# A hybrid convolution and attention layer on one core: another order of the first phase, and gate weights loaded beside the conv input

## The chip, the cores and the metric

The kernel runs on one core of a Trainium2 chip. The metric is the device time of one execution in microseconds (us). Before the change it was 634.33 us in the median of 3 runs (632.48 to 634.84). One further execution was recorded instruction by instruction; the profile and the trace are of that one.

The engines of the core, as the profile names them: PE (TensorE, matrix products; PEld is its weight load), DVE (VectorE), ACT (ScalarE), POOL (GpSimd) and SP (SyncE, which issues nearly all DMA transfers here). Each engine works through its own list of instructions in order. An instruction that waits holds back everything behind it on its engine, on SP a DMA issue as well.

## The reference

One layer with D = 1024, 1024 latent tokens (x) and 256 context tokens (ctx), all in float32:

```python
mod = silu(c) @ w_ada + b_ada                 # w_ada: 1024 x 3072
shift, scale, gate = split(mod, 3)            # adaLN; shift_c, scale_c likewise from c_ctx
hl = rmsnorm(x, norm_g) * (1 + scale) + shift
hc = rmsnorm(ctx, norm_g) * (1 + scale_c) + shift_c
zl = split(hl @ w_in)                         # w_in: 1024 x 3840, 11 parts
zc = split(hc @ w_in)                         # of it only keys and values are used
ya = zl[1] * dwconv3(zl[2] * zl[0]) * silu(zl[3])
yb = neighbourhood_attention(q=zl[4], k=zl[5], v=zl[6], keys and values of zc, rpb) * silu(zl[7])
yc = silu(layernorm(dwconv31(zl[8] * sigmoid(zl[9])) + b)) * silu(zl[10])
x  = x + gate * (concat(ya, yb, yc) @ w_out)
return rmsnorm(x, final_g)
```

The attention has 8 heads of 64, a window of 8 rows by 16 columns on a grid 64 wide with a bias per relative position, and all 256 context keys in the same softmax.

## The kernel before

**Precision.** A large product is made of three: an operand is split into a high half (a rounding copy, usually on ACT) and a low half (source minus high half, on DVE or POOL), and PE sums high x high, high x low and low x high in PSUM. In the code and in the profile these halves are `wh` and `wl` for weights, `h` (two tiles) for tokens.

**Stages.** In the first phase (`start()`, to 76.3 us) tokens are normalised, turned so that channels lie on the partitions, modulated and split; the first Q and K columns are multiplied there too. After it comes the conformer convolution's input for the first 128 of its channels ("the conv input", `cf_in(0)`: two weight blocks, each for two halves of the tokens, with matmuls at L325 to L327 and sinks at L667 and L670; the K columns of the context tokens stand behind its first half); then the v product (`v_proj`, L413 to L415, ten tiles of 128 tokens, to 162 us); then attention over four pairs of heads with the remaining projections between its rows; then the output product. The change touches the order of the first phase and three start times right behind it.

**The first phase is an order written by hand.** The string `SEQ` is read from left to right, and each word calls a small function in `start()` that issues some instructions. The letter names the function, the digits are its arguments:

| word | what it issues | lines |
|---|---|---|
| X0 to X9 | load of a tile of 128 tokens, 512 KB (0 to 7 latent, 8 and 9 context) | norm_load |
| L00 to L31 | load of adaLN weights, 1 MB in two transfers; k is a quarter of the columns, g a half of the rows | ada_load |
| W00 to W11 | load of 256 KB of `w_in` into a `wr` tile: i = 0 for the first Q columns, 1 for K; g is a half of the rows | L311 |
| w00 to w11 | split of such a tile: `wh` on ACT, then `wl` on POOL | L130, L131 |
| q50, q51 | sum of squares of token tile 5, on ACT (last digit 0) or on DVE (1) | L264, L266 |
| r42 | root of the mean square for tiles 4 and 5, on POOL | L270, L272 |
| x4 | scaling of token tile 4, on DVE | L960 |
| B00, B01 | adaLN product for quarter 0 with the first and with the second half of the rows, 4 matmuls each | L221 |
| R0, C0 | copy of that row to SBUF (ACT); 4 transposes (PE) and the small DVE steps that make `shift` and `scl` of quarter 0 | L226; L233, L235 to L241 |
| a0 to a7 | 4 transposes: 128 channels of token tiles 0 to 3 (a22: into a free `ps_z` tile) | L280 |
| b0 to b7, c0 to c3 | the same for tiles 4 to 7, and for the context tiles with 2 x 128 channels | L280 |
| f, g, h | modulation on ACT after a, b, c | L295 |
| u, v, o | split of the modulated tokens after f, g, h, both halves on DVE | L301, L302 |
| m0 to m7, n0 to n7 | 6 matmuls of Q and K for 128 channels: tokens 0 to 511 (m), 512 to 1023 (n) | L1010, L1011, L1013 |
| D16 | 16 warm-up matmuls of zeros into a tile (`po`) that is not yet in use | L980 |
| O, Q00 to Q12 | the attention tiles are allocated; Q and K are copied out of PSUM | L353, L354, L372, L373 |

In this phase the lists of PE, DVE, ACT, POOL and SP all follow the string. Behind it PE keeps the order of the code, and the lists of the other four are made by the framework's scheduler from the order of the code and added dependences. The buffers that matter: ten token tiles `x_in`, two PSUM tiles `ps_h` for transposes, two `ps_a` for adaLN rows, three `ps_z`, two `wr`, four pairs `wh`/`wl`.

**Behind the first phase** three side tasks run beside the conv input. `spawn(task, delay)` starts a task once the code has written out matmuls worth `delay` us by its own count (0.65 us for three matmuls of 512 columns, `mm_k`); a task then goes on whenever its next due time on that count is reached.

- `v_weights`: four loads of the v columns of `w_in` (L399) and their splits (ACT L130, DVE L131), 3.0 apart.
- `ada_gates`: the last third of `w_ada` in 16 loads of 256 KB (L810), each followed by one multiply and add on DVE (L815) that is bound to stand behind the PE instruction last written; 1.2 apart. At the end two splits and four transfers out to DRAM (L823). Each load takes a tile `t2`, of which there are four.
- `bias_first`: the position bias, as chains of small transfers through DRAM (tiles `dpr`, `dpm`, `u`) and tables loaded from them (L503).

The v product drains each token tile out of PSUM twice, by ACT (L424) and DVE (L425) into a `t2` tile, from the same four; the tile is then sent to DRAM (`vd`). Its PSUM tile is one of the three `ps_z`. DVE also does the 31 steps of the convolution (L681, L686) in that time.

Of the kernel before, what the change touches and what calls it, by code (L numbers as in the profile page):

```python
# [49 lines left out]

SEQ = """
X0 X1 X2 X3 L00 K L01 W00 W10 L10 L11 X4 X5 X6 X7 W01 W11 L20 L21 L30 L31 X8 X9
q00 q10 r02 x0 x1 q20 q30 r22 x2 x3 D16 a0 a1 a22 D04 B00 D04 B01 R0 D03 w00 w10 C0 D06
f0 f1 a3 u0 u1 m0 m1
B10 D04 B11 R1 D03 q40 q51 C1 D04 f2 f3 u2 u3 r42 x4 x5 m2 m3 q60 q71 r62 x6 x7 D04
b0 b1 g0 v0 g1 v1 B20 n0 b2 n1 b3 w01 w11 g2 v2 g3 v3 B21 R2 n2 a4 C2 n3 a5 f4 u4 f5 u5 b4
m4 B30 m5 b5 g4 v4 B31 g5 v5 R3 n4 a6 C3 a7 n5 f6 u6 f7 u7 b6 m6 b7 g6 v6 m7 g7 v7
q80 q90 r82 x8 x9 O Q00 n6 Q01 n7
c0 c1 h0 o0 h1 o1 c2 c3 h2 o2 h3 o3 Q02 Q10 Q11 Q12
"""  # L60


# [4 lines left out]
class Builder:  # L67
# [964 lines left out]
    def build(self):  # L1032
# [50 lines left out]
        self.t2 = e(self.pool("t2", 4, side="left"))  # L1083
        self.v_alloc()
        stv = ExitStack()
        self.spawn(self.v_weights(stv.enter_context(self.pool("vw", 1, side="right"))), 8.0)
        self.spawn(self.ada_gates(), 14.0)
        self.spawn(self.bias_first(), 16.0)
        first = self.cf_in(0)
        self.run(itertools.islice(first, KT), self.proj_pair(0, self.ws[1]), first)  # L1090
        self.conv = self.cf_conv()
# [101 lines left out]
```

## Time and profile before

| | |
|---|---|
| median of 3 runs | 634.33 us (632.48 to 634.84) |
| the profiled execution | 631.35 us |
| its span, first to last instruction | 629.6 us |
| PE busy | 600.2 us, 95% of the span |
| DVE, ACT, POOL busy | 399.8, 244.5, 180.4 us |
| granted PE clock, mean | 0.986 |
| DMA moved | 78.64 MB, 125 GB/s in the mean |

How to read the rows of the prediction. A row of the time line has a start in us from the span's first instruction, a length, the engine, the line of the code, the operation, output<-inputs by the names of the tiles, shapes, and how many instructions were put together (x4); in square brackets the idle time before it and what ended it. A row of the waits gives the waiting engine, tile and line, what it waited for, and then the sum in us, the count and the longest. A row of the windows gives, for each engine, busy us and the number of instructions, then the granted PE clock (1.00 is full speed), the busy share of the DMA engines and what they moved.

### The profile page before, as it was taken

What the parts mean: (1) busy time and instruction counts of PE and PEld (TensorE: products, weight loads), DVE (VectorE), ACT (ScalarE), POOL (GpSimd) and SP (SyncE); (2) the same over time, 40 slices, a digit from 0 to 9 for tenths busy, and PEclk for the clock granted to TensorE, in tenths of its full rate; (3) what the DMA queues carried; (4) which work ended last, traced back from release to release, by engine and by line L of the source; (5) the groups of instructions that cost most, each with busy time, mean ns of one, the idle gap of its engine ahead of it and who ended that gap; (6) DMA issues with size and microseconds to landing.
All of it is one profiled execution on the core that took longest, in us unless ns stands there. A gap on an engine that the chain in (4) does not pass through costs nothing.

```text
span 629.6 us, 8940 instructions
## 1 busy us (share of the span) xinstructions
PE 600.2 (95%) x3103; PEld 499.9 (79%) x3103; DVE 399.8 (64%) x681; ACT 244.5 (39%) x469; POOL 180.4 (29%) x199
## 2 busy tenths in 40 slices
PE   5879899999999999999999999999989999999995
PEld 4456688778879888888888888888878888888885
DVE  2365786688536679767799576754879636352333
ACT  4143751121144552455433455523645444231222
POOL 1121145000032331243232324312433270265112
PEclk9999799989999999999999999999999999999998
DMA  8991165885554114523127332163221255670122
GB/s 282 356 299 51 34 230 160 157 184 145 159 132 95 48 27 142 131 48 92 38 59 192 77 98 65 30 178 95 49 69 34 83 174 178 248 281 6 69 100 101
DMA packets 97170, 78.64 MB, mean 125 GB/s; under 512 B 26507, under 2 KB 80869, under 8 KB 96997
## 3 DMA queue, kind: packets, MB, share of 16 engines
q1 hardware_dynamic: 95397, 71.51, 40.5%
q10 hardware_dynamic: 1728, 6.55, 2.9%
q8 instruction: 25, 0.41, 0.3%
q14 instruction: 20, 0.16, 0.1%
HBM read 55.93 MB, written 14.29 MB: 112 GB/s over the span
## 4 chain that ended last, share of the span: by engine, by line
PE 79%; DMA 6%; DVE 5%; issue 3%; ACT 2%; POOL 2%; SPq 2%; DVEq 0%; POOLq 0%; ACTq 0%
PE ps_z L325 12%; PE ps_z L327 12%; PE ps_z L326 12%; PE po L621 5%; PE ps_t L609 5%; PE ps_f L869 5%; PE ps_f L870 5%; PE ps_f L868 5%; PE ps_s L590 4%; PE ps_s L591 2%; DMA t<-in_w_ada 2%; PE ps_z L413 2%; PE ps_z L414 2%; PE ps_z L415 2%; PE ps_h L280 2%
## 5 line engine op out<-in xcount | busy, mean ns | idle before, releaser
L325 PE MATMUL ps_z<-h,wh 128*128 128x512 f32 x384 | 151.8, 395 | 0.0
L327 PE MATMUL ps_z<-h,wl 128*128 128x512 f32 x384 | 150.8, 393 | 0.0
L326 PE MATMUL ps_z<-h,wh 128*128 128x512 f32 x384 | 150.2, 391 | 0.0
L131 POOL TENSOR_TENSOR wl<-wr,wh 128x512 fp32r<-128x512 f32 x52 | 75.1, 1447 | 121.2 <-ACT wh L130 106.9
L600 POOL TENSOR_SCALAR pr<-pr,sm 128x640 f32<-128x640 f32 (+1 forms) x64 | 52.9, 827 | 139.6 <-DVE sm L599 118.7
L327 PEld LDWEIGHTS ps_z<-h,wl 128*128 128x128 f32 x384 | 72.3, 188 | 16.4
L686 DVE SCALAR_TENSOR_TENSOR acc<-t,half_w,acc 128x1024 f32<-128x1024 f32 x60 | 81.8, 1363 | 1.1
L326 PEld LDWEIGHTS ps_z<-h,wh 128*128 128x128 f32 x384 | 72.5, 189 | 12.5
L325 PEld LDWEIGHTS ps_z<-h,wh 128*128 128x128 f32 x384 | 72.6, 189 | 12.2
L613 ACT ACTIVATE pw<-ps_t 128x640 fp32r<-128x640 f32 (+1 forms) x64 | 43.5, 679 | 91.1 <-PE ps_t L609 91.0
L595 DVE CUSTOM_DVE_ANT_0 ps_s<-ps_s,bt 128x640 f32<-128x640 f32 (+1 forms) x64 | 51.0, 796 | 35.5 <-PE ps_s L591 34.0
L614 DVE TENSOR_TENSOR pw<-ps_t,pw 128x640 fp32r<-128x640 f32 (+1 forms) x64 | 50.4, 788 | 17.2 <-ACT pw L613 16.9
L598 ACT ACTIVATE pr<-ps_s,mn 128x640 f32<-128x640 f32 (+1 forms) x64 | 49.0, 766 | 21.5 <-DVE mn L595 20.5
L621 PE MATMUL po<-pw,vt 128*128 128x256 f32 x304 | 51.3, 297 | 2.0 <-DVE yb L572 1.1
L869 PE MATMUL ps_f<-wol,y 128*128 128x512 f32 (+1 forms) x136 | 51.6, 379 | 0.0
L870 PE MATMUL ps_f<-woh,y 128*128 128x512 f32 (+1 forms) x136 | 51.5, 379 | 0.0
L868 PE MATMUL ps_f<-woh,y 128*128 128x512 f32 (+1 forms) x136 | 51.5, 379 | 0.0
L130 ACT ACTIVATE wh<-wr 128x512 fp32r<-128x512 f32 x52 | 32.5, 629 | 34.3 <-PE ps_z L326 27.5
L590 PE MATMUL ps_s<-kt,qd 128*128 128x384 f32 (+1 forms) x128 | 42.3, 351 | 1.7 <-DMA qd<-qn 1.2
L609 PE MATMUL ps_t<-ident,pr 128*128 128x128 f32 x304 | 43.6, 272 | 0.0
L621 PEld LDWEIGHTS po<-pw,vt 128*128 128x128 f32 x304 | 40.4, 189 | 3.8 <-issue 3.4
L609 PEld LDWEIGHTS ps_t<-ident,pr 128*128 128x128 f32 x304 | 36.0, 142 | 1.8 <-issue 0.9
(170 smaller groups left out, 916.5 us busy)
## 6 DMA issues: line engine op xcount, KB each, us to landing
wr<-in_w_in SPq DMA_DIRECT2D x52, 256.0 KB
wa<-in_w_ada SPq DMA_DIRECT2D x16, 512.0 KB
qd<-qn SPq DMA_DIRECT2D x32, 256.0 KB
vd<-t SPq DMA_DIRECT2D x20, 256.0 KB
x_in<-in_x SPq DMA_DIRECT2D x8, 512.0 KB
t<-in_w_ada SPq DMA_DIRECT2D x16, 256.0 KB
vt<-vd SPq DMA_DIRECT2D x32, 128.0 KB
fraw<-in_w_out SPq DMA_DIRECT2D x8, 512.0 KB
```

Source lines behind the costliest of these rows:

```text
L131: i2 = (eng or nc.vector).tensor_tensor(out=lo, in0=src, in1=f32(hi), op=ALU.subtract)
L325: nc.tensor.matmul(ps, lhsT=wh, rhs=hh, start=(k == 0), stop=False)
L326: nc.tensor.matmul(ps, lhsT=wh, rhs=hl, start=False, stop=False)
L327: self.last = nc.tensor.matmul(ps, lhsT=wl, rhs=hh, start=False, stop=(k == KT - 1))
L590: nc.tensor.matmul(win, lhsT=q[:, b % 4], rhs=kwin, start=(i == 0), stop=(i == 1))
L600: nc.gpsimd.tensor_scalar(out=pr, in0=pr, scalar1=sm, scalar2=0.5, op0=ALU.mult, op1=ALU.mult)
L609: nc.tensor.transpose(out=pt[:, c * P:(c + 1) * P], in_=pr[:, c * P:(c + 1) * P], identity=self.ident)
L621: self.nc.tensor.matmul(po, lhsT=vt[:, vi, h], rhs=pw[:, c], start=(c == 0), stop=(c == n - 1))
L686: self.after_pe(nc.vector.scalar_tensor_tensor(out=acc, in0=u[:, t:t + T], scalar=self.half_w[:, 2 * t + ct:2 * t + ct + 1], in1=acc, op0= ...
L868: nc.tensor.matmul(ps, lhsT=yh, rhs=wh[:, ch], start=(first and i == 0), stop=False)
L869: nc.tensor.matmul(ps, lhsT=yh, rhs=wl[:, ch], start=False, stop=False)
L870: nc.tensor.matmul(ps, lhsT=yl, rhs=wh[:, ch], start=False, stop=(last and i == len(chs) - 1))
```

## The change

Two things are changed: the string `SEQ`, and the delays of the three side tasks. The string has one line less, so every later line has a number smaller by one: L280 before is L279 after.

```diff
@@ -50,13 +50,12 @@
 SEQ = """
 X0 X1 X2 X3 L00 K L01 W00 W10 L10 L11 X4 X5 X6 X7 W01 W11 L20 L21 L30 L31 X8 X9
-q00 q10 r02 x0 x1 q20 q30 r22 x2 x3 D16 a0 a1 a22 D04 B00 D04 B01 R0 D03 w00 w10 C0 D06
-f0 f1 a3 u0 u1 m0 m1
-B10 D04 B11 R1 D03 q40 q51 C1 D04 f2 f3 u2 u3 r42 x4 x5 m2 m3 q60 q71 r62 x6 x7 D04
-b0 b1 g0 v0 g1 v1 B20 n0 b2 n1 b3 w01 w11 g2 v2 g3 v3 B21 R2 n2 a4 C2 n3 a5 f4 u4 f5 u5 b4
-m4 B30 m5 b5 g4 v4 B31 g5 v5 R3 n4 a6 C3 a7 n5 f6 u6 f7 u7 b6 m6 b7 g6 v6 m7 g7 v7
-q80 q90 r82 x8 x9 O Q00 n6 Q01 n7
-c0 c1 h0 o0 h1 o1 c2 c3 h2 o2 h3 o3 Q02 Q10 Q11 Q12
+q00 q11 r02 q20 x0 x1 q31 r22 x2 x3 D26 B00 a0 a1 a22 D02 B01 R0 D03 C0 D06
+f0 w00 f1 w10 a3 u0 u1 m0 m1
+B10 D02 B11 R1 D03 q40 C1 D04 f2 f3 q51 u2 u3 r42 q60 x4 x5 q70 r62 x6 x7 m2 m3 B20 D02
+b0 b1 g0 v0 g1 v1 w01 w11 n0 b2 n1 B21 R2 b3 g2 v2 g3 v3 n2 C2 a4 n3 f4 u4 a5 f5 u5
+b4 m4 B30 g4 v4 b5 g5 v5 q80 q90 B31 R3 m5 r82 n4 C3 a6 f6 x8 u6 a7 f7 x9 u7 n5 b6 m6 g6 v6 b7 m7 g7 v7
+O Q00 c0 c1 n6 h0 o0 h1 o1 c2 c3 Q01 n7 h2 o2 h3 o3 Q02 Q10 Q11 Q12
 """
@@ -1083,9 +1082,9 @@
-        self.spawn(self.v_weights(stv.enter_context(self.pool("vw", 1, side="right"))), 8.0)
-        self.spawn(self.ada_gates(), 14.0)
-        self.spawn(self.bias_first(), 16.0)
+        self.spawn(self.v_weights(stv.enter_context(self.pool("vw", 1, side="right"))), 2.0)
+        self.spawn(self.ada_gates(), 5.0)
+        self.spawn(self.bias_first(), 10.0)
```

No instruction is added or taken away; the 48 warm-up matmuls of the first phase are only placed otherwise. The loads (X, K, L, W) keep their order. The sums of squares of tiles 1 and 3 go from ACT to DVE, that of tile 7 from DVE to ACT.

The lists of three places follow. The first is PE at the head of the program, before: warm-up (L980), the first twelve transposes (L280), and behind them B00 and B01 (L221) with their transposes (L233).

```order
L980 MATMUL po<-zero,ones_r 128x512 x16
L280 MATMUL ps_h<-ident,x_in 128x128 x8
L280 MATMUL ps_z<-ident,x_in 128x128 x4
L980 MATMUL po<-zero,ones_r 128x512 x4
L221 MATMUL ps_a<-wa,stat 32x512 x4
L980 MATMUL po<-zero,ones_r 128x512 x4
L221 MATMUL ps_a<-wa,stat 32x512 x4
L980 MATMUL po<-zero,ones_r 128x512 x3
L233 MATMUL ps_a<-ident,ada_row 128x128 x4
```

The same place after the change:

```order
L979 MATMUL po<-zero,ones_r 128x512 x26
L220 MATMUL ps_a<-wa,stat 32x512 x4
L279 MATMUL ps_h<-ident,x_in 128x128 x8
L279 MATMUL ps_z<-ident,x_in 128x128 x4
L979 MATMUL po<-zero,ones_r 128x512 x2
L220 MATMUL ps_a<-wa,stat 32x512 x4
L979 MATMUL po<-zero,ones_r 128x512 x3
L232 MATMUL ps_a<-ident,ada_row 128x128 x4
```

B00 now stands ahead of the twelve transposes, with 26 warm-up products in front of it instead of 20. On ACT the two weight splits w00 and w10, which stood between R0 and f0, now stand behind f0 and f1.

The second place is PE at the end of the first phase, before: the matmuls of n6 and n7 (L1010 to L1013; the `h` tiles have numbers), the 16 context transposes (c0 to c3), and the first matmul of the conv input (L325).

```order
L1010 MATMUL ps_z<-h_78,wh 128x512
L1011 MATMUL ps_z<-h_78,wl 128x512
L1010 MATMUL po<-h_78,wh 128x512
L1011 MATMUL po<-h_78,wl 128x512
L1013 MATMUL ps_z<-h_79,wh 128x512
L1013 MATMUL po<-h_79,wh 128x512
L280 MATMUL ps_h<-ident,x_in 128x128 x16
L147 MATMUL ps_a<-ident,rows 128x74
L325 MATMUL ps_z<-h_78,wh 128x512
```

After the change, from the last matmul of n6 on:

```order
L1012 MATMUL po<-h_79,wh 128x512
L279 MATMUL ps_h<-ident,x_in 128x128 x8
L1009 MATMUL ps_z<-h_78,wh 128x512
L1010 MATMUL ps_z<-h_78,wl 128x512
L1009 MATMUL po<-h_78,wh 128x512
L1010 MATMUL po<-h_78,wl 128x512
L1012 MATMUL ps_z<-h_79,wh 128x512
L1012 MATMUL po<-h_79,wh 128x512
L146 MATMUL ps_a<-ident,rows 128x74
L324 MATMUL ps_z<-h_78,wh 128x512
```

Eight context transposes stand between n6 and n7, the other eight ahead of n6. The context tiles' squares, roots and scalings (q80 to x9) stand two lines of the string earlier, among n4 and n5.

The third place is DVE around the first drains of the v product, before: gate rows (L815; `t` and `stat` have numbers here), convolution steps (L686) and v drains (L425).

```order
L815 SCALAR_TENSOR_TENSOR acc<-t_982,stat_149,acc 128x512
L815 SCALAR_TENSOR_TENSOR acc<-t_994,stat_149,acc 128x512
L425 TENSOR_TENSOR t_997<-ps_z,t_997 128x4x64
L686 SCALAR_TENSOR_TENSOR acc<-t_736,half_w,acc 128x1024
L425 TENSOR_TENSOR t_1001<-ps_z,t_1001 128x4x64
L686 SCALAR_TENSOR_TENSOR acc<-t_736,half_w,acc 128x1024 x2
L815 SCALAR_TENSOR_TENSOR acc<-t_1013,stat_149,acc 128x512
L815 SCALAR_TENSOR_TENSOR acc<-t_1024,stat_149,acc 128x512
L686 SCALAR_TENSOR_TENSOR acc<-t_736,half_w,acc 128x1024
L815 SCALAR_TENSOR_TENSOR acc<-t_1034,stat_149,acc 128x512
L425 TENSOR_TENSOR t_1049<-ps_z,t_1049 128x4x64
```

After the change, from the second half of the conv input's product (L669) to the first v drain:

```order
L669 SCALAR_TENSOR_TENSOR t_736<-t_736,ps_z 128x512
L814 SCALAR_TENSOR_TENSOR acc<-t_953,stat_149,acc 128x512
L680 TENSOR_SCALAR acc<-t_736,half_w,convc 128x1024
L814 SCALAR_TENSOR_TENSOR acc<-t_964,stat_149,acc 128x512
L814 SCALAR_TENSOR_TENSOR acc<-t_973,stat_149,acc 128x512
L814 SCALAR_TENSOR_TENSOR acc<-t_988,stat_149,acc 128x512
L685 SCALAR_TENSOR_TENSOR acc<-t_736,half_w,acc 128x1024
L130 TENSOR_TENSOR t_999<-acc,t_998 128x512
L685 SCALAR_TENSOR_TENSOR acc<-t_736,half_w,acc 128x1024
L130 TENSOR_TENSOR t_1005<-acc,t_1004 128x512
L424 TENSOR_TENSOR t_1025<-ps_z,t_1025 128x4x64
```

All gate rows and the two splits of the gate (L130) now stand ahead of the first v drain.

## The prediction

> **What bounds the kernel now.** I read a table of stages first, to see where TensorE (PE) is not busy, then the list of PE's waits, then the time line around each wait.
>
> ```profile
> core 0: us, PE busy (x) PEld busy (x) DVE busy (x) ACT busy (x) POOL busy (x), PEclk, DMA share, GB/s
> 2.20:45.00 42.80, 32.94 (x151) 20.71 (x152) 17.19 (x36) 14.77 (x28) 6.47 (x11) 0.96 1.03 344
> 43.90:69.90 26.00, 26.00 (x148) 18.72 (x144) 16.34 (x32) 13.63 (x23) 5.36 (x5) 1.00 0.14 41
> 69.90:76.30 6.40, 3.98 (x18) 3.17 (x18) 5.52 (x8) 3.12 (x7) 1.27 (x1) 0.68 0.15 41
> 76.30:79.00 2.70, 2.70 (x8) 2.14 (x7) 2.61 (x9) 2.65 (x6) 0.16 (x2) 0.50 0.57 143
> 124.10:131.00 6.90, 4.04 (x12) 2.98 (x11) 3.72 (x6) 0.89 (x2) 0.00 (x0) 0.75 0.88 204
> 162.00:629.60 467.60, 455.56 (x2437) 390.25 (x2435) 293.48 (x523) 191.68 (x374) 150.35 (x158) 1.00 0.36 102
> ```
>
> From 162 us on PE is busy for 455.56 of 467.60 us; nothing that the change moves can gain there. What is open lies in the first phase (to 76.3 us), in the half clock behind it, and between 124 and 131 us. The waits say who is late:
>
> ```profile
> PE ps_h L280 <- DVE x_in L960: 8.0, 8, 2.3
> PE ps_z L413 <- DVE t L425: 2.9, 1, 2.9
> PE ps_h L280 <- ACT h_raw L295: 2.2, 2, 1.9
> ```
>
> The transposes (L280) wait for scaled token rows and for a free PSUM tile, and once the v product (L413) waits for its drain (L425). No wait behind the first two microseconds is for a load, although the DMA engines are full until 45 us (share 1.03, 344 GB/s).
>
> **Part 1, the head: adaLN products ahead of the transposes.**
>
> ```profile
> 12.39 1.42 DVE L960 TENSOR_SCALAR x_in<-x_in,ss 128x1024 f32<-128x1024 f32 x2 [1.86 <-POOL ss L272]
> 15.45 2.06 PE L980 MATMUL po<-zero,ones_r 128*128 128x512 f32 x4
> 17.43 1.11 PE L221 MATMUL ps_a<-wa,stat 128*32 128x512 f32 x8
> 19.61 1.07 PE L221 MATMUL ps_a<-wa,stat 128*32 128x512 f32 x8
> 20.74 0.60 ACT L226 ACTIVATE ada_row<-ps_a 128x512 f32<-128x512 f32 x1 [9.45 <-PE ps_a L221]
> 21.93 2.52 POOL L131 TENSOR_TENSOR wl<-wr,wh 128x512 fp32r<-128x512 f32 x2 [9.58 <-ACT wh L130]
> 22.39 0.86 DVE L239 TENSOR_TENSOR scl<-ada_t,modc 128x4 f32<-128x4 f32 x1
> 23.28 1.19 DVE L241 TENSOR_TENSOR scl<-scl,modc 128x4 f32<-128x4 f32 x1
> 33.90 0.16 DVE L241 TENSOR_TENSOR scl<-scl,modc 128x4 f32<-128x4 f32 x1
> 24.50 1.45 ACT L295 ACTIVATE h_raw<-ps_h,shift,scl 128x512 f32<-128x512 f32 x2 [2.13 <-DVE scl L241]
> 38.36 1.22 DVE L266 CUSTOM_DVE_ANT_0 sq<-x_in 128x1024 f32<-128x1024 f32 x1
> ```
>
> Before, the last of the first four token tiles was scaled at 13.81, and the adaLN products B00 and B01 stood behind its transposes and two rows of warm-up products, at 17.43 and 19.61. Now B00 stands in the gap before that tile is scaled, and the transposes a0 to a2 are queued behind it on PE. The first 3.1 MB (four x tiles and B00's weights) are in by about 12.5 us at 344 GB/s. Two of the four squares go to DVE; the second starts behind the first two scalings, so the last row comes some 0.5 us later (0 to one square, 1.3), at 14.3. Then 1.0 for the nine transposes left (0.11 each when warm, row at 42.23 below), two warm-up products 0.5 (half of the row at 15.45), B01 1.07 (weights in by 15 to 16.5): ada_row starts near 17.3, against 20.74. From there it was 1.65 to the small DVE steps, which took 0.86 and 1.19 while POOL ran two weight splits, and 0.16 when it did not. The splits w00 and w10 now stand behind f0 and f1, so f0 starts near 19.4 instead of 24.50, 5.1 earlier.
>
> Most of that is given back at once. m0 needs those splits, and they now end late: ACT does f0, w00, f1, w10 (2.8 together), POOL the second split by f0 + 4.2 (1.26 each, row at 21.93) to 5.0. So m0 and m1 end near 26 instead of 28.74, a gain of 2.7. The half split u0 and u1 runs on DVE beside POOL there.
>
> ```profile
> 43.87 0.69 DVE L302 TENSOR_TENSOR h<-h_raw,h 128x512 fp32r<-128x512 f32 x1
> 44.93 1.66 DVE L302 TENSOR_TENSOR h<-h_raw,h 128x512 fp32r<-128x512 f32 x1
> 44.65 1.40 POOL L131 TENSOR_TENSOR wl<-wr,wh 128x512 fp32r<-128x512 f32 x1 [3.92 <-ACT wh L130]
> ```
>
> A subtraction beside POOL's split took 1.66 instead of 0.69, so I count 1.0 for the meeting (0 to 2), within the 2.7. The Trainium skill ("SBUF — State Buffer", Who interferes with whom) goes further: a DVE instruction with two SBUF inputs and a GpSimd one that reads SBUF lock each other out for the whole instruction. By that rule both splits exclude both subtractions, 2 x 0.97 by the rows, and the total would come out about 1 us longer than mine; the row above agrees in kind.
>
> **Part 2, tokens 512 to 1023.**
>
> ```profile
> 28.74 1.07 PE L221 MATMUL ps_a<-wa,stat 128*32 128x512 f32 x8
> 40.76 1.42 DVE L960 TENSOR_SCALAR x_in<-x_in,ss 128x1024 f32<-128x1024 f32 x2 [1.17 <-POOL ss L272]
> 42.23 0.77 PE L280 MATMUL ps_h<-ident,x_in 128*128 128x128 f32 x5 [0.33 <-DVE x_in L960]
> 43.92 0.50 PE L1010 MATMUL ps_z<-h,wh 128*128 128x512 f32 x1
> ```
>
> B10 starts 2.7 earlier, and two warm-up products less (0.5) make it 3.2 at f2 (0.03 behind the row at 33.90, now 30.9). Before, q71 stood on DVE behind x4 and x5; now q60 and q70 run back to back on ACT behind f3: 30.9 + 1.45 + 2 x 1.25 + 1.0 on POOL = 35.8, then 1.42 for x6 and x7: 37.2 instead of 42.18. On DVE the square q51, moved behind C1, costs 1.30 ahead of u2 and is hidden: x4 and x5 end at 35.9. B20 now covers the wait for x6 (its weights end at 10.5 MB, some 33 us); n0 then waits 1.0 for g0 and v0, bare. n0 starts near 38.9 instead of 43.92: **gain 5.0** (2.5 to 6).
>
> **Part 3, context tokens among the second half.**
>
> ```profile
> 69.83 2.48 DVE L960 TENSOR_SCALAR x_in<-x_in,ss 128x1024 f32<-128x1024 f32 x2 [1.98 <-POOL ss L272]
> 72.36 1.75 PE L280 MATMUL ps_h<-ident,x_in 128*128 128x128 f32 x7 [1.40 <-DVE x_in L960]
> 74.42 2.03 PE L280 MATMUL ps_h<-ident,x_in 128*128 128x128 f32 x8 [0.31 <-ACT h_raw L295]
> 76.31 0.78 PE L325 MATMUL ps_z<-h,wh 128*128 128x512 f32 x1
> ```
>
> Between 69.9 and 76.3 PE does 16 transposes and waits. They now stand ahead of n6 and n7, at a warm clock: 16 x 0.11 (spacing in the row at 42.23) = 1.8. **Gain 4.6** (3 to 4.6). The cover is PE's own 26 us of products: DVE, busy 16.34 of them, takes on x8, x9 (1.42) and part of four hc splits (4 x 1.12), some 22 of 28 us. Without that cover up to 1.6 us of the old waits (4.6 to 3.0) come back. The squares q80 and q90 now take 2.5 us of ACT ahead of R3; two products of 1.4 stand between B31 and C3 on PE and hide it; bare it would cost those 2.5, which the lower bound of the sum's range takes in. The 2.7 us at clock 0.50 behind the pause also go: **gain 1.35** (0 to 1.35).
>
> One wait is new. The second weight split of the conv input stood at 69.78 on ACT, before the first L325.
>
> ```profile
> 78.20 0.60 ACT L353 ACTIVATE qn<-ps_z 128x512 fp32r<-128x512 f32 x1
> 69.78 0.63 ACT L130 ACTIVATE wh<-wr 128x512 fp32r<-128x512 f32 x1
> 70.49 1.27 POOL L131 TENSOR_TENSOR wl<-wr,wh 128x512 fp32r<-128x512 f32 x1 [0.70 <-ACT wh L130]
> ```
>
> Now it stands behind three Q copies of 0.60, so about 1.8 us after the first L325; with 0.63 on ACT and 1.27 on POOL, up to 1.0 more beside DVE, its low half is there at +3.7 to 4.7, and PE wants it at +3.2. Behind it on PE stands the whole conv input. **Cost 1.0** (0 to 2).
>
> **Part 4, gate weights beside the conv input.**
>
> ```profile
> 86.38 2.00 DVE L131 TENSOR_TENSOR wv<-yb,wv 128x1024 fp32r<-128x1024 f32 x1 [0.24 <-ACT wv L130]
> 106.22 0.97 SPq L810 DMA_DIRECT2D t<-in_w_ada  x2
> 111.17 1.54 DVE L815 SCALAR_TENSOR_TENSOR acc<-t,stat,acc 128x512 f32<-128x512 f32 x2 [1.04 <-DMA t<-in_w_ada]
> 126.11 0.75 DVE L815 SCALAR_TENSOR_TENSOR acc<-t,stat,acc 128x512 f32<-128x512 f32 x1 [2.18 <-DMA t<-in_w_ada]
> 127.34 0.76 PE L413 MATMUL ps_z<-wv,h 128*128 128x512 f32 x1 [2.86 <-DVE t L425]
> ```
>
> The gate rows and the v drains share four t2 tiles. The last gate row held the second v tile's drain to 127.2, while PE wanted its PSUM buffer at 124.5: 2.86 idle, and with the clock at 0.75 over 6.9 us (half speed for 3.4, idle part left out) 1.5 more. Now all 16 gate rows and the two splits stand ahead of the first drain. Counted from the first L325: rows 1 to 4 at +9.7 to +13.6, around the last split of the v weights (86.38, which was +10.1); a refill takes 3.3 to 5 (106.22 to 111.17, table loads in front); rows 5 to 9 to +18.5. Rows 10 to 12 wait in DVE's order for the first half of the conv product (+20.3), 13 for the second (+25.9), so 16 ends near +31; the splits, their way out to DRAM (3.3 to 5) and two convolution steps let the first v tile drain at +37 to +41.5. PE wants that buffer at +25.7 + 3 x 5.5 = +42.2. So the stall goes, by a margin of 1 to 5: **gain 4.4** (0 to 4.4). The wr loads that SP now issues behind gate rows are wanted at +15 and +18, and issued by +4.1. The wait of 1.4 for qd at 174.7 stays (-1.4 to 1.4).
>
> **Sum.** 5.0 + 4.6 + 1.35 - 1.0 + 4.4 = 14.35. Span 629.6 - 14.35 = 615.25; with 1.75 around it (631.35 in all) 617.0. That execution was 2.98 under the median 634.33, so I forecast 620.0 beside that median.
>
> **The rivals.** (A) The loads set the pace: the DMA engines are full to 45 us whatever the order, so an earlier head only waits for the next weights. Then part 1 and 2 keep 1 of their 5.0: 634.33 - 10.35 = 624.0. For it: share 1.03. Against it: no PE wait for a load, and the last weights (B31, in by 43.7) are wanted near 50. (B) The v drain is late again, one tile earlier, because SP sends the gate's way out behind a weight load and a table load: part 4 keeps 0: 634.33 - 9.95 = 624.4. For it: the margin of 1 to 5. Against it: most table loads now stand behind the gate rows. (C) Slower: the four t2 tiles refill one at a time, 12 x 5 = 60 us from +10, as happens if each gate load waits behind a table load on SP. The first drain then comes at +70 + 8 and PE stands 36 us at L413, 1.5 more for the clock: 634.33 - 9.95 - 4.4 + 37.5 = 657. It decides from a first drain past +55 (42.2 + 14.35 - 1.5): each 1 us beyond is a loss. For it: the row at 111.17. Against it: SP has 13 of the 16 gate loads ahead of the first u table.
>
> **How the numbers follow.** Forecast 0.60, A 0.12, B 0.20, C 0.04, and 0.04 for A, B and a PE wait in part 3 together, which ends near 630 to 633. The forecast's own range, by the bounds above, is 615 to 625; with A and B whole it is 614.5 to 627. A measurement of this kernel can tell about 0.5% (3.2 us) from no change: faster 0.93, same 0.03 (the mixed case), slower 0.04 (C).
>
> **What would show it.** Right: f0 near 19, n0 near 39, first L325 near 67 with clock 1.00 behind it, a PE pause of about 1 us 3 us later, no pause at L413, and the rest a shifted copy. Part 1 is wrong if B00 waits for its load beyond 14 us; part 2 if x6 is scaled after 39; part 3 if c0 or n7 waits for DVE or ACT; part 4 if L413 waits, most likely at the fourth v tile. I would be wrong as a whole if the first L325 moved by less than 5 us.

## The result and the profile after

The changed kernel takes 618.51 us in the median of four runs (618.29 to 619.25). The kernel before, run beside it, took 633.4 (four runs, 631.99 to 634.84). The ratio is 0.977, with a 95% interval of 0.974 to 0.979: faster by 2.3%, 14.9 us. The profiled execution took 618.29 us, its span is 616.5.

The forecast was 620.0 with a range of 614.5 to 627.0, so the time lies inside it, 1.5 under the forecast. Not every term was right, as the two traces show when the same instruction is looked up in both. Times are us from the start of the span. "This stage gave" is what was gained since the row above.

| instruction | before | after | earlier by | this stage gave | predicted |
|---|---|---|---|---|---|
| n0, first matmul of tokens 512 to 1023 | 43.92 | 41.05 | 2.87 | 2.87 | 5.0 |
| first matmul of the conv input | 76.31 | 69.87 | 6.44 | 3.57 | 4.6 |
| first matmul of the v product | 102.32 | 95.44 | 6.88 | 0.44 | 1.35 - 1.0 |
| last matmul of the v product | 161.80 | 150.60 | 11.20 | 4.32 | 4.4 |
| first attention product | 176.32 | 163.76 | 12.56 | 1.36 | 0 |
| last matmul | 622.27 | 609.21 | 13.06 | 0.50 | 0 |

The table of stages of the kernel after, with the columns of the table that the prediction shows of before:

```profile
2.20:41.00 38.80, 32.55 (x146) 20.12 (x146) 17.53 (x35) 12.35 (x24) 7.71 (x10) 0.96 1.04 342
41.00:69.80 28.80, 27.49 (x160) 20.39 (x161) 20.20 (x39) 16.72 (x30) 5.52 (x7) 1.00 0.25 81
69.80:73.50 3.70, 3.52 (x16) 2.55 (x14) 3.57 (x8) 3.51 (x6) 1.00 (x1) 1.00 0.98 343
110.00:118.00 8.00, 7.74 (x35) 6.05 (x34) 7.46 (x9) 2.02 (x5) 4.72 (x7) 1.00 0.90 188
151.00:616.50 465.50, 455.04 (x2436) 390.13 (x2435) 292.57 (x523) 191.75 (x374) 149.85 (x158) 1.00 0.36 103
```

The pause with 3.98 busy of 6.40 us ahead of the conv input is gone, and so is the half clock behind it (1.00 where it was 0.50). Around the drain of the v product (110 to 118) PE is busy for 7.74 of 8.00 us. From 151 us on the rest is nearly the copy that it was forecast to be; 0.4 of the 0.50 in the last row of the first table is one wait (for a tile `t` at L728, in all 1.1 before and 0.7 after). What stays open lies ahead of 41 us, where PE is busy for 32.55 of 38.80 us, and in 1.3 us between 41.0 and 69.8.

From PE's waits in the kernel after (engine, tile, line, what for; sum, count, longest):

```profile
PE ps_z L1009 <- DVE h L300: 3.5, 3, 1.3
PE ps_a L220 <- DMA wa<-in_w_ada: 1.1, 1, 1.1
PE ps_z L1010 <- POOL wl L130: 1.6, 2, 1.3
PE ps_z L326 <- POOL wl L130: 0.5, 1, 0.5
PE ps_z L412 <- DVE t L424: 0.3, 1, 0.3
```

The 8.0 us of waits for scaled tokens are gone. In their place stand waits for split tokens (L300), for the low halves of w00 and w10 (L130), and one for a load: B00 (L220) waits for its weights. The wait for the v drain went from 2.9 to 0.3, and stands at the fourth v tile now.

The time line of the kernel after shows where these lie:

```profile
13.85 1.06 PE L220 MATMUL ps_a<-wa,stat 128*32 128x512 f32 x8 [1.08 <-DMA wa<-in_w_ada]
18.01 0.60 ACT L225 ACTIVATE ada_row<-ps_a 128x512 f32<-128x512 f32 x1 [7.33 <-PE ps_a L220]
20.04 0.78 ACT L294 ACTIVATE h_raw<-ps_h,shift,scl 128x512 f32<-128x512 f32 x1 [1.44 <-DVE scl L240]
21.42 3.13 POOL L130 TENSOR_TENSOR wl<-wr,wh 128x512 fp32r<-128x512 f32 x2 [8.30 <-ACT wh L129]
22.04 1.38 DVE L300 CAST h<-h_raw 128x512 fp32r<-128x512 f32 x1
23.18 0.64 PE L1010 MATMUL ps_z<-h,wl 128*128 128x512 f32 x1 [1.29 <-POOL wl L130]
23.45 1.64 DVE L301 TENSOR_TENSOR h<-h_raw,h 128x512 fp32r<-128x512 f32 x1
27.89 1.06 PE L220 MATMUL ps_a<-wa,stat 128*32 128x512 f32 x8
...
45.60 0.60 ACT L225 ACTIVATE ada_row<-ps_a 128x512 f32<-128x512 f32 x1 [3.36 <-PE ps_a L220]
46.10 1.44 ACT L294 ACTIVATE h_raw<-ps_h,shift,scl 128x512 f32<-128x512 f32 x2
47.38 0.50 PE L1009 MATMUL ps_z<-h,wh 128*128 128x512 f32 x1 [1.26 <-DVE h L300]
...
73.84 0.50 PE L326 MATMUL ps_z<-h,wl 128*128 128x512 f32 x1 [0.52 <-POOL wl L130]
...
112.37 0.47 PE L412 MATMUL ps_z<-wv,h 128*128 128x512 f32 x1 [0.26 <-DVE t L424]
```

f0 starts at 20.04, 4.46 earlier than before. Behind it both splits on POOL take 3.13 (1.71 and 1.45 by the single rows; 2.52 before), the cast of u1 takes 1.38 (0.42 before) and its subtraction 1.64 (0.69 before). PE waits for POOL there (1.29 at 23.18), not for u1. B10 starts at 27.89, only 0.85 earlier. At 47.38 n2 waits 1.26 us: the modulation it needs (L294 at 46.10) stands on ACT behind R2 (L225 at 45.60), which waits for B21. That wait was not in the prediction.

### The profile page after: what moved, and what is told of

It is laid out like the page before. It is cut to its first block, busy times and chain, and to the rows that moved or that the text cites. A ratio compares the mean times of both kernels' runs of the same rounds, so it can differ in the third digit from the quotient of the medians.

```text
span 616.5 us, 8946 instructions
## 1 busy us (share of the span) xinstructions
PE 595.5 (97%) x3103; PEld 496.7 (81%) x3103; DVE 399.7 (65%) x683; ACT 243.0 (39%) x467; POOL 177.7 (29%) x199
## 3 DMA queue, kind: packets, MB, share of 16 engines
q1 hardware_dynamic: 95397, 71.51, 41.5%
## 4 chain that ended last, share of the span: by engine, by line
PE 82%; DMA 5%; DVE 3%; ACT 3%; issue 2%; SPq 2%; POOL 2%; POOLq 0%; DVEq 0%; ACTq 0%
PE ps_z L324 13%; PE ps_z L326 13%; PE ps_z L325 13%; PE po L620 6%; PE ps_t L608 5%; PE ps_f L868 5%; PE ps_f L869 5%; PE ps_f L867 5%; PE ps_s L589 4%; DMA wr<-in_w_in 3%; PE ps_s L590 2%; DMA t<-in_w_ada 2%; PE ps_z L412 2%; PE ps_z L414 2%; PE ps_z L413 2%
## 5 line engine op out<-in xcount | busy, mean ns | idle before, releaser
L325 PE MATMUL ps_z<-h,wh 128*128 128x512 f32 x384 | 149.7, 390 | 0.0
L130 POOL TENSOR_TENSOR wl<-wr,wh 128x512 fp32r<-128x512 f32 x52 | 71.4, 1376 | 132.8 <-ACT wh L129 104.3
L325 PEld LDWEIGHTS ps_z<-h,wh 128*128 128x128 f32 x384 | 72.2, 188 | 12.4
L589 PE MATMUL ps_s<-kt,qd 128*128 128x384 f32 (+1 forms) x128 | 42.2, 350 | 0.5 <-ACT pr L597 0.4
```

The costliest lines, as they stand in the source:

```text
L130: i2 = (eng or nc.vector).tensor_tensor(out=lo, in0=src, in1=f32(hi), op=ALU.subtract)
L325: nc.tensor.matmul(ps, lhsT=wh, rhs=hl, start=False, stop=False)
L589: nc.tensor.matmul(win, lhsT=q[:, b % 4], rhs=kwin, start=(i == 0), stop=(i == 1))
```

## The experiments

Twelve kernels were run, each timed beside the kernel before. Medians of the kernel before were 632.2 to 632.9 in these groups, over single runs from 628.5 to 635.9. The ratios are against it. Their intervals are some 0.3% to each side, 2 us, so where two experiments differ by less than that, the traces are what tells them apart.

**The order alone.** The three start times are put back.

```diff
-        self.spawn(self.v_weights(...), 2.0)
-        self.spawn(self.ada_gates(), 5.0)
-        self.spawn(self.bias_first(), 10.0)
+        self.spawn(self.v_weights(...), 8.0)
+        self.spawn(self.ada_gates(), 14.0)
+        self.spawn(self.bias_first(), 16.0)
```

> The new order of the first phase with the three start times of before (8, 14 and 16). Theory (the parts add up): the v product starts as early as after the change (95.4 us against 102.3), the stall of L412 for the v drain is back with its half clock (4.2 between the two traces), and so is the wait of 1.4 for qd: 618.5 + 4.2 + 1.4 = 624.1, about 9 under before. Rival 1 (the stall shrinks by itself, because an earlier phase leaves the drains more time): at most 1 us of wait at L412 and 619 to 621. Rival 2 (the order gives nothing without the start times): over 629.

Measured: 624.8 us, ratio 0.989 (0.986 to 0.992). The v product starts at 94.36, 8.0 earlier than before. The stall (PE waiting at L412 until DVE has drained a tile of the v product) is back, at the fifth v tile as before, with a wait of 2.0 where it was 2.9 and a clock of 0.74 in the 6.5 us behind it. So is the wait of 1.2 for `qd`, the query tile of the first attention product, which a DMA transfer brings. The theory holds; the stall does not go by itself.

**The start time of the gate rows alone, with the new order.** The v weights start at 8 and the bias task at 16 again, the gate rows stay at 5.

> The new order, and of the three start times only that of the gate weights (5); v weights 8 and bias 16 as before. Theory (the gate rows alone held the drain's tiles): no stall over 0.5 us at L412, and the wait for qd of 1.4 comes back if it hung on the start of the bias task: 618.5 to 620.0. Rival (the three start times work only together, since gate loads now queue on the sync engine among v weights and table loads): gate rows end more than 4 us later, the stall is back at least in part: 621.5 to 624.

Measured: 619.06, ratio 0.981 (0.978 to 0.983). There is no wait for the v drain at all, and the wait for qd is back with 1.3. So the gate rows are what held the drain's tiles.

**The start times alone, with the old order.** The string `SEQ` of before.

> The order of before with the three new start times (2, 5, 10). Theory (the parts add up): the stall at L413 goes (4.2) and the wait for qd too (1.4), the first phase stays as it was: 633.4 - 5.6 = 627.8. Rival (the earlier loads meet the first phase: v weights and gate rows take the DMA and the vector engine while context tokens are still split): the first matmul of the conv input comes later than 76.3 us or it waits for its weights, and the time is 630 or more.

Measured: 628.21, ratio 0.994 (0.992 to 0.996). By the time the theory looks right (627.8), by the trace it is not. Two of the kernel's waits (it has the line numbers of before):

```profile
PE ps_h L280 <- DVE x_in L960: 7.1, 7, 2.0
PE ps_z L413 <- DVE t L425: 2.9, 1, 2.9
```

The stall of 2.9 is still there, only one v tile earlier. The wait for qd is gone. What this execution gained beside that lies elsewhere: the first matmul of the conv input came at 73.55, 2.76 earlier than before, with a clock of 1.00 ahead of it and behind it. Of this, 1.86 stands already at n0 (42.06 against 43.92), in a part that has the same order in both kernels and differs in the clock (1.00 against 0.77 from 13.5 to 21 us). The profiled execution is also the fastest of twelve (625.04 to 631.45). So the agreement of the median with 627.8 is luck: of its two terms one came.

**The context tokens in their old place.**

```diff
-... g5 v5 q80 q90 B31 R3 m5 r82 n4 C3 a6 f6 x8 u6 a7 f7 x9 u7 n5 ...
-O Q00 c0 c1 n6 h0 o0 h1 o1 c2 c3 Q01 n7 h2 o2 h3 o3 Q02 ...
+... g5 v5 B31 R3 m5 n4 C3 a6 f6 u6 a7 f7 u7 n5 ...
+q80 q90 r82 x8 x9 O Q00 n6 Q01 n7
+c0 c1 h0 o0 h1 o1 c2 c3 h2 o2 h3 o3 Q02 ...
```

> The change with its third part undone: context tokens squared, scaled, transposed and split behind n7 again, start times and the rest of the order as after. Theory (the transposes and their waits are what is saved, 3.6 between n0 and the first matmul of the conv input in the two traces, and the half clock 1.35, less the wait of 0.5 for the second weight split): 618.5 + 3.6 + 1.35 - 0.5 = 622.9, with a clock of 0.50 behind the pause. Rival (the 3.6 came from elsewhere, for instance from the first rows of the second half, and the context tokens hide in the old place as well): within 1 us of 618.5. Sharper: 3.6 is less than the 4.6 I had priced, because n2 waits 1.3 for the modulation that stands behind the adaLN row R2 on the scalar engine; if that wait belongs to another part, undoing this one costs 4.6 + 1.35 - 0.5 = 5.4 and gives 623.9.

Measured: 625.97, ratio 0.990 (0.988 to 0.993), slower than both versions of the theory. The stage behind the first phase in this kernel, by the table of stages, and then its wait at the v drain (its string is one line longer, so its lines are numbered as before the change):

```profile
74.00:78.00 4.00, 3.75 (x14) 3.11 (x13) 3.93 (x11) 3.60 (x8) 0.16 (x2) 0.57 0.29 87
```

```profile
PE ps_z L413 <- DVE t L425: 3.3, 1, 3.3
```

From n0 to the first matmul of the conv input it takes 33.16 us against 28.82 in the change: the third part is worth 4.34 there, and the half clock is back (0.57 from 74 to 78). But the stall at the v drain is back too, with 3.3, although the gate rows start at 5. So with these start times the fourth part works only together with the third. This and the run with the start times alone left a question: what makes the drain late there?

**The place of the bias task.** In both kernels with a late drain, the order of the sync engine's queue (SP) differs from the change in a few places. One of them is tried here: the last of the 16 gate loads stands behind the second load of a `u` table, not ahead of it. Starting the bias task 1 us earlier does this to the change. It is not a test of that place alone: a few other transfers trade places too, and in the two kernels a further table load stands among the four transfers that carry the gate out to DRAM (`gd`), which this run does not repeat.

```diff
-        self.spawn(self.bias_first(), 10.0)
+        self.spawn(self.bias_first(), 9.0)
```

> The change with the bias task started at 9 instead of 10. On the sync engine the last gate load then stands behind the second bias table load instead of ahead of it, as it does in the two kernels (order of before with new start times; context tokens in the old place) in which the stall at the v drain stayed whole. Theory (that one place decides: the last gate row comes 4 to 5 us later, and with it the splits, the transfers out and the first drain): a wait of 2 to 3 us at the fourth v tile, with half a clock behind it 4 us in all, 622 to 623. Rival (the stall stayed there because the context splits keep the vector engine busy behind the first matmul of the conv input, and the place on the sync engine is of no account): no wait over 0.6 there, 618.5 to 619.

Measured: 618.69, ratio 0.979 (0.976 to 0.982). The last gate row and the fourth v tile in this kernel:

```profile
105.69 0.75 DVE L814 SCALAR_TENSOR_TENSOR acc<-t,stat,acc 128x512 f32<-128x512 f32 x1 [0.95 <-DMA t<-in_w_ada]
...
114.25 0.47 PE L412 MATMUL ps_z<-wv,h 128*128 128x512 f32 x1 [1.38 <-DVE t L424]
```

The time is the rival's. A wait of 1.38 is there, between the theory (2 to 3) and its rival (under 0.6). Counted from the first matmul of the conv input, the last gate row comes at +35.0 instead of +32.3, but the drain only 1.1 later. The time line of the change shows why: there something else already holds the second gate split on ACT (t<-acc).

```profile
98.99 0.82 SPq L445 DMA_DIRECT2D u<-dpr  x1
99.86 3.39 SPq L310 DMA_DIRECT2D wr<-in_w_in  x2
102.28 0.63 ACT L129 ACTIVATE t<-acc 128x512 fp32r<-128x512 f32 x1 [16.43 <-DVE acc L814]
105.49 0.63 ACT L129 ACTIVATE wh<-wr 128x512 fp32r<-128x512 f32 x1 [2.57 <-DMA wr<-in_w_in]
106.31 0.63 ACT L129 ACTIVATE wh<-wr 128x512 fp32r<-128x512 f32 x1 [0.19 <-DMA wr<-in_w_in]
106.85 0.62 ACT L129 ACTIVATE t<-acc 128x512 fp32r<-128x512 f32 x1
```

Two weight splits stand between the two gate splits, and the first of them waits 2.57 us for its load, which stands behind a table load on SP. Issuing it takes SP from 99.86 to 103.25 (the row is for two loads). The opposite step starts the task at 12:

> The change with the bias task started at 12 instead of 10. On the sync engine one weight load of the conv input's second block then stands ahead of the last gate rows' table loads, and on the scalar engine one weight split instead of two stands between the two gate splits. Theory (the first drain of the v product hangs on the sync queue: in the change the second gate split waits behind two weight splits whose load was issued 2.9 late behind a table load): the first v tile is drained 2 to 4 us earlier than 111.8 (counted from the first matmul of the conv input at 69.9), no wait for the drain; since the wait was only 0.3 in the change, 617.8 to 618.3, with less scatter. Rival (the tables then come too late): the wait for qd of 1.4 is back, 619.3 to 619.7.

Measured: 618.53, ratio 0.978 (0.976 to 0.981). Of the theory and of the rival a part came true. The drain has margin again, with no wait, but its step was another than the theory's: two weight splits still stand between the two gate splits, and the first still waits 3.25 us for its load. All of it comes earlier: counted from the first matmul of the conv input, SP starts on that load at +27.4 instead of +30.0, the second gate split starts at +35.3 instead of +37.0, and the drain ends 1.7 earlier (2 to 4 forecast). And the wait for qd is back:

```profile
PE ps_s L589 <- DMA qd<-qn: 1.5, 1, 1.5
```

Put together over all kernels with the gate rows at 5: when the second drain of the first v tile ends, counted from the first matmul of the conv input (PE wants that buffer at about +42.2), and how long it is from the last v matmul to the first attention product.

| bias task starts at | drain of the first v tile | wait at L412 | to the first attention product |
|---|---|---|---|
| 9 | +43.4 | 1.4 | 13.16 |
| 10 (the change) | +42.4 | 0.3 | 13.16 |
| 10 (four variants of the first phase, below) | +42.9, +44.0, +43.1, +43.2 | 0.8, 1.9, 1.0, 1.1 | 13.16 |
| 11 | +42.8 | 0.8 | 13.25 |
| 12 | +40.6, +39.6 | 0 | 14.83, 13.86 |
| 16 | +38.8 | 0 | 14.63 |

The change stands on the edge: by the traces, starting the tables earlier costs 1.1 us at the drain, and starting them later 0.7 to 1.7 ahead of the first attention product. The medians do not tell the three start times 9, 10 and 12 apart (618.69, 618.51, 618.53). What makes the drain later still in the two kernels with the whole stall (+45.7 with the context tokens in their old place, +44.2 with the old order) is not settled.

**The splits w00 and w10 back ahead of f0.**

```diff
-... B01 R0 D03 C0 D06
-f0 w00 f1 w10 a3 u0 u1 m0 m1
+... B01 R0 D03 w00 w10 C0 D06
+f0 f1 a3 u0 u1 m0 m1
```

> The change, with one piece of its first part undone: the two weight splits w00 and w10 stand between R0 and C0 again, ahead of f0 and f1; B00 stays early. Theory (moving them gave nothing, because m0 needs them anyway, and behind f0 they meet the token splits and leave PE a gap of 1.3 at 22 us in which the clock falls to 0.50 for 3.3 to 6.7 us): f0 about 1.5 later than 20.0, m0 begins near 23 and runs without a gap, m1 ends near 26.5 instead of 27.9 at a clock of 1.00: 1 to 2 us under the change, 616.5 to 617.5. Rival (the move is what gave the earlier f0, 2.9 of it at n0): f0 and with it m0 and n0 come 1.5 to 2.5 later than after the change, 620 to 621.

Measured: 617.33, ratio 0.976 (0.973 to 0.979), not to be told from the change by the time. In this kernel:

```profile
19.79 0.86 DVE L238 TENSOR_TENSOR scl<-ada_t,modc 128x4 f32<-128x4 f32 x1
20.69 1.19 DVE L240 TENSOR_TENSOR scl<-scl,modc 128x4 f32<-128x4 f32 x1
21.91 1.45 ACT L294 ACTIVATE h_raw<-ps_h,shift,scl 128x512 f32<-128x512 f32 x2 [2.12 <-DVE scl L240]
```

f0 starts 1.87 later than in the change, yet m2 and n0 come 1.72 earlier (n0 at 39.33 against 41.05), with a clock of 1.00. The move of the splits, then, is no gain but a loss. About 1.1 of it is the half clock of the profiled execution of the change: in that of the order alone, with the splits moved and a clock of 1.00, n0 comes at 39.99. The other 0.7 is the later end of the two splits, which on POOL take 3.13 behind f0 and 2.51 ahead of it. At the v drain 0.8 us of wait takes part of it back.

**Five more warm-up products ahead of m0**, in the gap of 1.29 us at 22 us (`a3 u0 u1 D05 m0 m1`).

> The change with five more warm-up products ahead of m0, in the time in which PE otherwise waits for the first low weight half (21.9 to 23.2 us). Theory (the wait itself costs nothing, the half clock that follows it does, 3.3 us of it in the trace of the change and 6.4 to 6.7 in two other executions with the same head): m1 ends about 1 earlier, at 26.9, with a clock of 1.00 throughout: 1 to 2 us under the change, 616.5 to 617.5. Rival (the low halves set the pace, the clock is of no account there): m1 ends at 27.9 and the time is 618.5; or the products themselves are in the way and it is 619.

Measured: 618.38, ratio 0.978 (0.975 to 0.981). The table of stages of this kernel:

```profile
20.00:31.00 11.00, 9.85 (x50) 5.31 (x49) 4.16 (x4) 3.79 (x6) 3.15 (x2) 1.00 1.08 368
```

The clock is 1.00 (0.84 in the change over the same 11 us), and n0 and the conv input come 1.09 earlier. That the five products did this is not shown: the execution of the order alone has none of them, a clock of 1.00 too, and n0 at the same place (39.99, here 39.96). The time does not move: the drain of the v product stays where it was (112.8 against 112.2), and PE waits 1.9 us there. This gain in the head is worth nothing, since the drain has no margin.

**B00 back behind the transposes.**

```diff
-... x2 x3 D26 B00 a0 a1 a22 D02 B01 R0 ...
+... x2 x3 D16 a0 a1 a22 D04 B00 D04 B01 R0 ...
```

> The change with the other piece of its first part undone: B00 stands behind the twelve transposes again, with the warm-up products of before (16 ahead, 4 and 4 around B00); the splits stay behind f0 and f1. Theory (the early B00 is what the head gains: of the 4.46 by which f0 came earlier, 1.8 belong to the splits' place, as the run with the splits back shows, and the other 2.7 to B00): f0 at 22 to 22.7 instead of 20.0, m1 and n0 2 to 2.7 later, so 620.5 to 621.2. Rival (the two squares that went to the vector engine give the 2.7, and B00 only fills a gap that was there): f0 within 0.7 of 20.0 and 618.5 to 619.

Measured: 623.06, ratio 0.986 (0.983 to 0.988). The head of this kernel, by the time line and by the table of stages:

```profile
14.29 0.47 PE L279 MATMUL ps_h<-ident,x_in 128*128 128x128 f32 x1 [3.15 <-DVE x_in L959]
18.77 1.78 PE L220 MATMUL ps_a<-wa,stat 128*32 128x512 f32 x8
22.76 0.60 ACT L225 ACTIVATE ada_row<-ps_a 128x512 f32<-128x512 f32 x1 [11.86 <-PE ps_a L220]
```

```profile
13.50:21.00 7.50, 6.52 (x24) 3.83 (x25) 1.40 (x2) 0.00 (x0) 0.00 (x0) 0.55 1.12 334
```

ada_row comes at 22.76 instead of 18.01, n0 at 44.81 instead of 41.05. So 3.76 us at n0 hang on B00 with its 26 warm-up products ahead, more than the theory's 2.7: without them PE pauses for 3.15 us ahead of the transposes and runs at a clock of 0.55 to 21 us. The edit moves both, so what belongs to the place of B00 and what to the ten warm-up products is not separated.

**R2 behind g2.**

```diff
-... n1 B21 R2 b3 g2 v2 g3 v3 n2 ...
+... n1 B21 g2 v2 R2 b3 g3 v3 n2 ...
```

> The change with the adaLN row R2 behind the modulation g2 on the scalar engine instead of ahead of it. Theory (n2 waits 1.26 for g2, which stands behind R2, which waits for B21): that wait goes, 1.3 less at the first matmul of the conv input, 617.2. Rival 1 (the vector engine is next, since POOL still splits weights until 44.9 beside it): 0.3 of the 1.3 comes, 618.2. Rival 2 (PE lacks work later: C2 and with it f4 come no earlier, so the wait moves to m4 or n4): 618.5.

Measured: 616.58 (616.16 to 619.54), ratio 0.977 (0.973 to 0.980). From n0 to the first matmul of the conv input it takes 27.39 us against 28.82: the wait of 1.26 is gone and nothing takes its place. At the v drain 1.1 us of wait eats most of it, so by the time it is not to be told from the change.

**A version built on these.** The splits ahead of f0, R2 behind g2, the bias task at 12, and the squares and scalings of tokens 512 to 1023 as early as their loads land, with b0 and b1 among m2 and m3. Only the lines of the squares are shown:

```diff
-f0 w00 f1 w10 a3 u0 u1 m0 m1
-B10 D02 B11 R1 D03 q40 C1 D04 f2 f3 q51 u2 u3 r42 q60 x4 x5 q70 r62 x6 x7 m2 m3 B20 D02
-b0 b1 g0 v0 g1 v1 w01 w11 n0 ...
+f0 f1 a3 u0 u1 q40 q51 r42 m0 m1
+q60 x4 x5 q71 r62 B10 D02 B11 R1 D03 C1 D04 f2 f3 x6 x7 b0 u2 u3 g0 v0 m2 b1 g1 v1 m3 w01 w11 B20
+n0 ...
```

> A version built on the findings: splits w00 and w10 ahead of f0, R2 behind g2, bias task at 12, and the squares, roots and scalings of tokens 512 to 1023 as early as their loads land (ahead of R1 on the scalar engine, in idle time of the vector engine), with b0 and b1 among m2 and m3 and B20 behind them. Theory (each wait is its own price: 1.7 for the splits with the clock, 1.3 for R2, 1.8 for the early squares at n0, 0.3 to 1 at the v drain): the first matmul of the conv input near 65 instead of 69.9, no wait at the drain, 613 to 614.5. Rival 1 (the drain stays where it is in absolute time, because the gate rows wait for loads): the gain at the conv input is eaten by a wait of 2 us and more at L412, 616 to 617. Rival 2 (loads: tiles 6 and 7 land near 28, and the scalar engine waiting for them holds R1 and with it everything): n0 later than 39.3, 617 or more.

Measured: 615.9 (614.91 to 617.07), ratio 0.975 (0.972 to 0.977). The conv input starts at 66.41, 3.46 earlier than in the change, and there is no wait at the drain. The theory had 65 and 613 to 614.5, so it was too hopeful by 1.4 us both times. By the medians it beats the change by 2.6 us; the intervals of the two ratios overlap, so "better than the change" is likely, not shown. A last step, 12 instead of 6 warm-up products behind C0 and the bias task at 11:

> The version with early squares, with six more warm-up products behind C0 (12 instead of 6, in the 1.9 us in which PE waits there for f0) and the bias task at 11 instead of 12. Theory (the wait at 20 to 22 us costs only through the half clock behind it, 3.3 us of it in that version's trace; and the bias task decides the wait for qd, 13.5 us from the end of the v product to the first attention product there against 12.8 with the task at 10): clock 1.00 in the head, n0 near 38 instead of 39.0, 0.7 less before the first attention product, 614 to 614.8 against 615.9. Rival (the sixteenth gate load goes behind a table load again and the drain of the fourth v tile is late): a wait of 1 to 2 us at L412 takes it back, 615.5 to 616.5.

Measured: 616.22, ratio 0.975 (0.972 to 0.978): no gain, and the rival's time. The clock is 1.00 in the head (0.84 in the version before this, from 20 to 31 us), and the adaLN row (R1) is copied 0.77 earlier (29.08 against 29.85). But the square of the last token tile (30.82 below) waits 0.32 for its load, and the adaLN steps behind it on DVE start 0.45 later than in the version before. At the drain 0.8 us is back.

```profile
28.03 1.06 ACT L263 ACTIVATE sq<-x_in 128x1024 f32<-128x1024 f32 x1 [1.41 <-DMA x_in<-in_x]
30.82 1.23 DVE L265 CUSTOM_DVE_ANT_0 sq<-x_in 128x1024 f32<-128x1024 f32 x1 [0.32 <-DMA x_in<-in_x]
```

The wait of 1.41 on ACT, for the load of another token tile, stands in both versions.

## Why the prediction was right, and where it was not

**The whole.** Measured against the profiled executions the gain was 13.1, the sum said 14.35. Two errors met: the sum was 1.25 too large, and the step from the profiled execution to the median was 2.98 in the forecast and 0.22 in the result (618.51 against 618.29). They have opposite signs, so part of the closeness of 620.0 to 618.51 is luck. The executions of before scatter over 7 us, the four of the change over 1. The range of 615 to 625 is also not what the bounds of the terms add up to: taken all at their lower or all at their upper end they give a gain of 2.1 to 17.75, which is 632.2 to 616.6 from the median.

**Part 1 failed at this step:** "So m0 and m1 end near 26 instead of 28.74, a gain of 2.7". B10 came at 27.89, a gain of 0.85, so 1.9 is missing. Three things make it up.

First, f0 came at 20.04 where 19.4 was forecast. The prediction had B00's weights in by about 12.5; B00 waited for them until 13.85. The transposes queued behind it on PE were over at 16.1 (15.3 forecast), and ada_row came at 18.01 (17.3 forecast). Second, the half clock behind the gap of 1.29 us was not in the sum at all. It cost about 1.0, as the execution of the order alone shows, which has the same head, a clock of 1.00 and B10 at 26.82. The last 0.2 lies between f0 and B10 in that execution too (6.83 us, 6.6 forecast).

The meeting on DVE and POOL was not the step that failed. The cast and the subtraction of u1 were held up by 1.9 together, but PE did not wait for them. PE waited for the low halves from POOL, and the second of these was there 4.5 after f0, inside the 4.2 to 5.0 forecast. The Trainium skill ("SBUF — State Buffer", Who interferes with whom) was the reason for a total 1 us longer. Its rule agrees in kind with the rows (u1's subtraction 1.64 instead of 0.69, POOL's two splits 3.13 instead of 2.52). That 26.82 at full clock is also 0.8 behind the 26 forecast does not confirm the price: 0.6 of this is f0.

The reason given for the gain was right where it spoke of B00 (3.8 us at n0 by the run without it, the warm-up products included) and wrong where it spoke of the splits. Their move brings f0 forward by 1.87, as argued, but costs 0.7 at n0 at full clock, and 1.7 in the profiled execution of the change.

**Part 2** was forecast to add 2.3 and added 2.0: x6 was scaled from 37.91 (35.8 forecast), with most of the delay from part 1, and n0 waited 0.90 for its split tokens (1.0 forecast).

**Part 3.** The moved transposes are worth 4.34 by the run that undoes them, 4.6 forecast. The stage shows only 3.57 because n2 waits for g2 behind R2: the prediction went through the moved squares on ACT and passed over R2, which the new string puts ahead of g2. Half clock less the new wait for the weight split was 0.35 forecast and 0.44 measured. That it fits hides two sizes that were both too large: the wait was 0.52 where 1.0 stood, so the half clock was worth 0.96 where 1.35 stood.

**Part 4.** 4.32 measured, 4.4 forecast. The forecast let the first v tile drain at +37 to +41.5, and PE wants it at +42.2: it came at +42.4. So the margin of 1 to 5 was none, and that the wait was 0.26 and not 1 to 2 is luck. Rival B, which the prediction held for one case in five, is false for the change itself. It came true in part in the six variants that wait 0.8 to 1.9 there, and whole in the two that put back the old order or the old place of the context tokens. The series of start times points to the mechanism that it named (the gate's way out behind a weight load and a table load on SP); a run that changes that queue alone was not made.

**What was counted at nothing.** The wait for qd was put at 0 with bounds of 1.4 to each side, and the upper bound came: 1.36. The traces show why. Before, three table loads (`bt`) stand on SP directly ahead of the first transfer of qd; after, it is issued 6.73 us behind the last v matmul instead of 8.65:

```profile
168.12 2.23 SPq L503 DMA_DIRECT2D bt<-u  x3
170.45 0.68 SPq L360 DMA_DIRECT2D qd<-qn  x1
```

```profile
157.33 1.34 SPq L359 DMA_DIRECT2D qd<-qn  x2
```

The run with the bias task at 12 brings the wait back.

**Rival A** (loads set the pace) is false for the change as a whole: beyond 14 us PE waits for no load there. But the first step of the head does hang on one: B00 waited for its load until 13.85, and until 14.04 and 14.15 in two of the variants, just past the mark of 14 that the prediction had set for part 1. In the last two versions, where the waits ahead are taken away, ACT and DVE wait for token loads (1.41 and 0.32 in the rows above).

## What to carry to other kernels

Parts of a change are not worth their sum: here each half alone left the stall at the drain in place (0.6% and 1.1% against 2.3% together), and gains ahead of a consumer with no margin were eaten by it. Where a forecast rests on a margin, follow every in-order queue that feeds it to the end, that of the DMA issues above all, and ask what 1 us more does. When work is moved behind an instruction on the same engine, list everything in between in the new order, the rows that do not move too: an instruction that waits, as R2 did here for B21, holds what stands behind it.

## What the runs showed that was not expected

The same head, gap for gap, ran at different clocks in different executions. Three rows, of the change, of the order alone, and of the gate rows alone:

```profile
23.20:26.60 3.40, 3.06 (x7) 1.94 (x8) 1.86 (x2) 0.00 (x0) 1.34 (x1) 0.53 1.03 404
```

```profile
23.20:26.60 3.40, 2.71 (x11) 1.84 (x11) 1.81 (x2) 0.00 (x0) 1.30 (x1) 1.00 1.04 406
```

```profile
23.20:30.60 7.40, 6.83 (x20) 3.32 (x20) 1.84 (x2) 0.00 (x0) 1.32 (x1) 0.54 1.06 376
```

Behind a gap of 1.3 us the clock fell to half for 3.4 us, not at all, or for 7 us, which moves n0 by up to 2.7 us (39.99 to 42.72). The Trainium skill ("TensorE: Matmul & The Clock Gate", Part 1) says that PE's clock gate judges its activity in free-running windows of about 3.4 us. The lengths here agree with one window and two, and that they vary agrees with a window that does not start with the kernel; why so short a gap is enough, no run here shows. The length of the gap alone does not decide: with a gap of 1.89 us ahead of f0's first products the clock from 20 to 31 us was 1.00 in two kernels (that of before, and the one with the splits put back), and with a gap of 1.90 it was 0.84 in a third (the early squares). The profiled executions of both kernels with warm-up products in the gap had a clock of 1.00, but so had two of the seven with the head of the change and without them, so that they keep the clock up is likely, not shown.
